# An encoder block on one Trainium2 core: when VectorE applies a norm's gain and bias, and when it prepares one pair of hidden tiles

## The chip, the core and the metric

The kernel runs on one core of a Trainium2 chip. The metric is the device time of one execution in microseconds: 1099.08 us is the median of three runs of the kernel before (1098.75 to 1099.74).

The engines are named as in the profile: PE is TensorE (PEld its weight loads), DVE VectorE, ACT ScalarE, POOL GpSimd, SP the engine whose queue issues the DMAs.

## The reference, cut to what matters

One post-norm transformer layer on 256 tokens of width 2048, all in float32:

```python
mix = hybrid_mixer(x, ...)
x = layer_norm(ALPHA * x + mix, ln1_g, ln1_b)
mem_n = layer_norm(mem, mem_ln_g, mem_ln_b)
xa = memory_cross_attention(x, mem_n, ...)
x = layer_norm(ALPHA * x + xa, ln2_g, ln2_b)
ff = jnp.square(jax.nn.relu(x @ w_mlp_in)) @ w_mlp_out     # 2048 -> 8192 -> 2048
x = layer_norm(ALPHA * x + ff, ln3_g, ln3_b)
```

The change lies in the MLP `ff` and in the residual `ALPHA * x`, where x is the second norm's output.

## The kernel before, in words

**Precision.** A float32 weight is used as the sum of a high and a low half. `queued_split` (L954) makes the halves of a piece of 1024 (or 512) columns: ScalarE writes the high half `w_hi` (L955), VectorE the low half `lo` as weight minus high half (L956). A product is three matmuls (`mm3`, L163): L164 takes the high half, L165 the low half, L166 the high half with the low half of the other operand. The high halves have a ring of four buffers (`wsp`), the low halves four fixed ones.

**Hidden tiles and units.** The hidden layer has 64 tiles of 128 columns. The first eight are made in two *groups of column tiles* (`hidden_group`, L977), four at a time; each group reads eight pieces of weights, and after each piece of the second group `pump` takes two entries from the list `side`. All other tiles come from `hidden_tile` (L1009), one at a time: two pieces of weights (`part`, L958), per piece eight matmuls with the high half and eight with the low half. Two neighbouring tiles are a *pair*. A *unit* ("u", c, q, p) multiplies pair p of chunk c with its rows of the second weight matrix, for half q of the output columns. There are four chunks (c) and two halves (q): eight passes (`one_pass`, L1060) of eight units. Units 0 to 5 of all passes but the last use seven products in place of eight: one unit has four parts (1024, 512, 1024 and 1024 columns) and 21 matmuls, and needs sums of weight blocks (`push_sums`, L942, three VectorE operations into `s_t`) and sums of the pair's blocks. Units 6 and 7 use plain products.

**A pair's steps.** `stages` (L877) returns four: x1 `square` (ScalarE: relu and square, L883, L884), x2 `halve` (ScalarE L874, VectorE L875), x3 `add` (VectorE L894, L897, L898: the sums of blocks), x4 `halve_sums` (L874, L875 again, on the sums). Below, a1 to a4 and b1 to b4 are those of a group's first and second pair. Ahead of them each tile is evacuated from its bank (`evacuate`, L868: ScalarE L870, VectorE L871).

**The order of items.** `items` (L908) lists tiles and units: in the pass (0, 0) tiles 8, 9, unit 0, tile 10, unit 1, tile 11, unit 2, and so on; in later passes a tile ahead of each unit at first. The tiles made in pass (c, 1) belong to the next chunk. `fetch` (L919) loads each item's 1 MB of weights into a ring of buffers: four, and five from the item `JOIN` on, when the buffer `row_b` joins. Before, JOIN is unit 5 of the pass (0, 1).

**What sets the order on an engine.** `queue` (L105) chains an instruction to the one queued before it on the same engine: queued instructions run in the order in which they are emitted. What is not queued is free, and is put between the others by the scheduler. Splits, matmuls, the sums of weight blocks and the row operations are queued; merges, evacuations of single tiles and the steps of most pairs are free. `part` takes work from three lists after each split: from `banks` if there is any, and then from `sums`, or, if that is empty, from `banks` or `side` (`pump`, L114).

**The row operations.** `norm_ops(q)` (L1183) multiplies the residual `res[b]`, both blocks b of 128 tokens, by the gain of the second norm and adds its bias, for 1024 columns: four VectorE operations of 128x1024 (L1186). Their rows come into `row_b` by two DMAs (`norm_rows`, L1178). Half 0 is needed before the first pass' results are merged into `res`, half 1 before the second's. Before, half 0 was done in `side`: two operations in the second group, two in the first pass (`rows[2:]`), then the loads of half 1, whose four operations were in `side` at the start of the pass (0, 1).

**Merges.** When a pass' six seven-product units are done, `banks` gets eight operations (L1126) that add the accumulated products `p1, p5, p6, p7` into `res`; they are taken by the parts of the last two tiles and of unit 6. The four x accumulators are merged at the end of the pass (L1152).

**A pair in a pass.** After its second tile, `hidden_tile` puts the pair's four steps into `late_finish` (L1036); they are emitted after the next unit, or ahead of the next tile, whichever comes first, and are free except for the last pair of a chunk.

Of the kernel before, what the change touches and what calls it, by code (L numbers as in the profile page):

```python
# [15 lines left out]
ALU = mybir.AluOpType  # L16
# [22 lines left out]
def encoder_kernel(ctx: ExitStack, tc: tile.TileContext, t, out):  # L39
# [24 lines left out]
    def acc_tile():  # L64
        return psA.tile([P, 512], F32, tag="acc", name="acc")

    def att_tile():
        return psT.tile([P, 512], F32, tag="att", name="att")
# [33 lines left out]
    side, banks, fixed_lo = deque(), deque(), deque()  # L102
# [174 lines left out]
    cq = attA[:, 6144:8192].rearrange("p (k c) -> p k c", c=512)  # L277
# [178 lines left out]
    for b in range(NB):  # L456
# [3 lines left out]
        a, c, e = krn[:, 0:64], krn[:, 64:128], krn[:, 256:512]  # L460
        nc.vector.tensor_tensor(out=a, in0=v, in1=krt[:, 0, b, :], op=ALU.mult)
        for i in range(2):
            j = 1 - i
# [372 lines left out]
    LEAD = CH // 2  # L836
# [8 lines left out]
    m_t = late.tile([P, 512], F32, name="m_t")  # L845
# [62 lines left out]
    items = []  # L908
    for c, q in PASSES:
# [3 lines left out]
        for u in us:  # L913
            n = 2 if q == 0 and u[3] == (CH // 2 - 2 if c else 0) else 1
            items += gs[:n] + [u]
            gs = gs[n:]
    JOIN = items.index(("u", 0, 1, 5))

    def fetch():  # L919

# [7 lines left out]
        elif n:  # L928
            raws.append(row_b if n == JOIN else raws[n - (4 if n < JOIN else 5)])
        raw = raw_of[it] = raws[n]  # L930
# [4 lines left out]
        nc.sync.dma_start(raw, src)  # L935
        if n == JOIN:
            fetch()
# [39 lines left out]
    def hidden_group(nexts, tiles, c, j0, beside=None):  # L977
# [22 lines left out]
        def empty(i, h):  # L1000
            for j in range(2):
                evacuate(outs[2 * i + j], h, j, queue)

        todo = [stages(h, c, j0 // 2 + i, queue) for i, h in pairs]
        return [lambda i=i, h=h: empty(i, h) for i, h in pairs], todo

    now, late_finish = [], []

    def hidden_tile(it, ps):  # L1009

        _, c, j = it
        for h_ in range(2):
            hi, lo = part(raw_of[it][:, h_ * 1024:(h_ + 1) * 1024])
            k0 = 8 * h_

            def w_hi(k):
                queue(nc.tensor.matmul(ps, hi[:, k * P:(k + 1) * P], x2t[:, k0 + k, :],  # L1017
                                       start=k0 + k == 0, stop=k0 + k == KT - 1))

            for k in range(7):  # L1020
                w_hi(k)
            if h_ == 0:
                w_hi(7)
            for k in range(8):
                queue(nc.tensor.matmul(ps[:, 0:S], lo[:, k * P:(k + 1) * P], x2t[:, k0 + k, 0:S],  # L1025
                                       start=False, stop=False))
            if h_ == 1:
                w_hi(7)
        if j % 2 == 0:
            now[:] = [tmp_tile()]  # L1030
        evacuate(ps, now[0], j % 2)
        if j % 2:
            def rest(h=now[0]):
                for stage in stages(h, c, j // 2, queue if j == CH - 1 else free_order):
                    stage()
            late_finish.append(rest)  # L1036

    bank = []
    at = [0]
# [20 lines left out]
    def one_pass(c, q):  # L1060
# [17 lines left out]
        r11, r12, r21, r22 = [res[b][:, cc] for b in range(NB) for cc in cols]  # L1078
# [3 lines left out]
        def merge(r, x, op=ALU.add):  # L1082
            if any(r is y for y in fresh):
                fresh[:] = [y for y in fresh if y is not r]
                nc.vector.scalar_tensor_tensor(out=r, in0=r, scalar=ALPHA, in1=x, op0=ALU.mult, op1=op)
            else:
                nc.vector.tensor_tensor(out=r, in0=r, in1=x, op=op)  # L1087

        def more(ps, op=ALU.add):
            nc.vector.tensor_tensor(out=m_t, in0=m_t, in1=ps, op=op)  # L1090

        spare, n_seven, n_unit, parts = [], 0, 0, []
        while n_unit < len(order):
            it = step()
            if it[0] == "g":
                if n_unit == 0:
                    ps = {LEAD: x22, LEAD + 1: x21}[it[2]] if it[1] == 0 else p6
                elif n_seven < len(sevens):
                    ps = x22
                else:  # L1100
                    spare = spare or [p1, p6]
                    ps = spare[0]
                    spare.reverse()
                hidden_tile(it, ps)
                continue
            p, raw, k = it[3], raw_of[it], 2 * it[3]
            n_unit += 1
            if p in sevens:
                if n_seven == 0:
                    while banks:  # L1110
                        banks.popleft()()
                while sums:
                    sums.popleft()()
                for src, todo in ((raw[:, 512:1536], ((p1, a(c, k, 0)), (x12, sm(c, p, 3)))),
                                  (raw[:, 1536:2048], ((x11, a(c, k + 1, 0)),)),
                                  (s_t[:, 0:1024], ((p5, sm(c, p, 1)), (p7, sm(c, p, 0)))),
                                  (s_t[:, 1024:2048], ((p6, sm(c, p, 2)), (x21, a(c, k + 1, 1))))):
                    for (hi, lo), (ps, x) in zip(halves(part(src)), todo):
                        mm(ps, x, hi, lo)
                n_seven += 1  # L1120
                if at[0] < len(items) and is_seven(items[at[0]]):
                    push_sums(items[at[0]])
                if n_seven == len(sevens):
                    nc.scalar.activation(m_t, p1, AF.Copy)

                    banks.extend([lambda: merge(r11, m_t), lambda: more(p6),  # L1126
                                  lambda: merge(r12, m_t, ALU.subtract), lambda: more(p7, ALU.subtract),
                                  lambda: merge(r21, m_t), lambda: merge(r22, m_t, ALU.subtract),
                                  lambda: merge(r22, p5), lambda: merge(r12, p5)])
            elif final and len(order) - n_unit < HELD:  # L1130
                n = len(parts) // 2
                for i in range(2):
                    o = (2 * n + i) * 1024
                    lo = sums_h[2 * n + i - 1] if n + i else lo_tile()
                    w = halves(part(raw[:, i * 1024:(i + 1) * 1024], wide[:, o:o + 1024], lo))
                    parts.append((k + i, w))
                    for (hi, lo), ps in zip(w, (x12, x11)):
                        mm(ps, a(c, k + i, 0), hi, lo)
            else:
                for i in range(2):  # L1140
                    w = halves(part(raw[:, i * 1024:(i + 1) * 1024]))
                    for (hi, lo), to in zip(w, ((x12, x22), (x11, x21))):
                        for b in range(2):
                            mm(to[b], a(c, k + i, b), hi, lo)
            if q == 1:
                give("h", c, p)
                if p in SEVEN:
                    give("s", c, p)
            if late_finish:
                late_finish.pop()()  # L1150
# [27 lines left out]
    def norm_rows(q):  # L1178
        for i, w in enumerate("gb"):
            nc.sync.dma_start(row_b[:, i * 1024:(i + 1) * 1024],  # L1180
                              t[f"ln2_{w}"][q * 1024:(q + 1) * 1024].partition_broadcast(P))

    def norm_ops(q):  # L1183
        o = q * 1024
        return [lambda i=i, b=b, op=op: queue(
            nc.vector.tensor_tensor(out=res[b][:, o:o + 1024], in0=res[b][:, o:o + 1024],  # L1186
                                    in1=row_b[:, i * 1024:(i + 1) * 1024], op=op))
            for i, op in enumerate((ALU.mult, ALU.add)) for b in range(NB)]

    for g in range(LEAD // G):  # L1190
        empty, (first, second) = hidden_group((lambda k: w_mi0[k // 2]) if g == 0 else (lambda k: s_in.next()),
                     att_tile if g % 2 else acc_tile, 0, g * G, first_pair if g == 0 else None)
        wait = [lambda: None]

        def both(*todo):
            return [lambda: [x() for x in todo]]

        if g == 0:
            norm_rows(0)
            rows = norm_ops(0)  # L1200
            (a1, a2, a3, a4), (b1, b2, b3, b4) = first, second
            side.extend(wait * 4 + empty + [a1, b1, a3, a2, a4, b3, b2, rows[0], b4, rows[1]])
            s_in.split, s_in.beside = queued_split, 2
        else:
            (a1, a2, a3, a4), (b1, b2, b3, b4) = first, second
            assert not side
            side.extend(wait + both(*empty) + [a1] + both(a3, a2) + [a4, b1] + both(b3, b2) + [b4] + rows[2:] + [lambda: norm_rows(1)])
    bank[:] = [acc_tile() for _ in range(4)] + [att_tile() for _ in range(4)]
    for cq in PASSES:
        if cq == (0, 1):  # L1210
            side.extend(norm_ops(1))
        one_pass(*cq)

    g3, b3 = s_t, raw_of[items[-5]]
# [137 lines left out]
```

## Time and profile before

| What | Value |
|---|---|
| three runs, median (lowest, highest) | 1099.08 us (1098.75, 1099.74) |
| the profiled execution's time | 1098.77 us |
| its span, first to last instruction | 1097.0 us |
| granted TensorE clock over the span | 0.996 |
| groups of column tiles (MLP's start) | from about 399 us |
| passes (0, 0) and (0, 1) | from 446.6 and 535.5 us |
| row operations (L1186) | 439.2 to 547 us |

The times in the trace count from the first instruction. In timelines a row gives start, duration (of several merged instructions together), engine, line, operation, what is written and read, the count, and in brackets the idle time of the engine just before, with what ended it. In groups (x count) the numbers are the busy time in total, the mean of one in ns, and idle time. VectorE's rows overlap a little: an instruction begins before the one before it has ended.

### The profile page before, as it was taken

The page shows a single profiled execution, that of the slowest core. Times are in us where ns is not written, and L with a number is a line of the kernel's source. Part 1 is how long each engine was busy: PE and PEld are TensorE (multiplying, and loading weights), DVE is VectorE, ACT ScalarE, POOL GpSimd, SP SyncE. Part 2 cuts the span into 40 slices and gives each one's busy share as a digit, 9 for nine tenths or more (in the row PEclk, how much of TensorE's full clock was granted, in tenths as well). Part 3 has the DMA queues.
Part 4 walks back from the last instruction along what each step waited for, and adds up shares of the span by engine and source line. Part 5 has one row for each costly group of instructions (what it writes and reads, how often), then busy time and mean ns, then how long its engine had stood idle before and what let it go on. Part 6 is the DMA issues. An engine that isn't in the chain of part 4 may idle for free.

```text
span 1097.0 us, 15276 instructions
## 1 busy us (share of the span) xinstructions
PE 1078.5 (98%) x5864; PEld 932.4 (85%) x5864; DVE 936.8 (85%) x1299; ACT 638.4 (58%) x925; POOL 35.6 (3%) x45
## 2 busy tenths in 40 slices
PE   9999999999999999999999999999999999999996
PEld 6988899988999878878888888888888888888885
DVE  6878677678879677899999999899999899999876
ACT  6555566546576426657567557466566566666640
POOL 2402000000100000000000000000000000000000
PEclk9999999999999999999999999999999999999998
DMA  9664453466567444555565555646546555655632
GB/s 330 243 230 137 152 192 135 159 244 224 183 221 251 145 148 172 194 209 197 190 242 207 203 186 201 220 168 223 201 183 229 193 192 202 220 180 194 250 143 78
DMA packets 37369, 215.87 MB, mean 197 GB/s; under 512 B 4272, under 2 KB 5168, under 8 KB 13616
## 3 DMA queue, kind: packets, MB, share of 16 engines
q1 hardware_dynamic: 37296, 214.89, 55.0%
q8 instruction: 46, 0.75, 0.3%
q14 instruction: 27, 0.22, 0.1%
HBM read 212.78 MB, written 2.10 MB: 196 GB/s over the span
## 4 chain that ended last, share of the span: by engine, by line
PE 93%; DVE 5%; ACT 1%; issue 1%; DMA 0%; POOL 0%; DVEq 0%; SPq 0%
PE acc L164 13%; PE acc L165 13%; PE acc L166 13%; PE acc L1017 12%; PE acc L1025 6%; PE att L1017 6%; PE att L165 4%; PE att L166 4%; PE att L164 4%; PE att L1025 3%; PE acc L206 2%; PE acc L204 2%; PE acc L205 2%; DVE lo L956 1%; PE acc L213 1%; PE att L213 1%
## 5 line engine op out<-in xcount | busy, mean ns | idle before, releaser
L88 DVE TENSOR_TENSOR w_lo<-raw,w_hi 128x1024 fp32r<-128x1024 f32 (+2 forms) x130 | 147.4, 1142 | 60.1 <-ACT w_hi L87 59.1
L87 ACT ACTIVATE w_hi<-raw 128x1024 fp32r<-128x1024 f32 (+2 forms) x134 | 131.5, 989 | 114.3 <-PE acc L166 71.6
L956 DVE TENSOR_TENSOR lo<-raw,w_hi 128x1024 fp32r<-128x1024 f32 (+1 forms) x154 | 171.3, 1130 | 9.1 <-ACT w_hi L955 8.8
L955 ACT ACTIVATE w_hi<-raw 128x1024 fp32r<-128x1024 f32 (+1 forms) x154 | 147.6, 983 | 29.8 <-PE acc L166 26.3
L1017 PE MATMUL acc<-x2t,w_hi 128*128 128x512 f32 x592 | 153.3, 391 | 0.0
L1017 PEld LDWEIGHTS acc<-x2t,w_hi 128*128 128x128 f32 x592 | 108.9, 189 | 19.6
L956 DVE TENSOR_TENSOR lo<-s_t,w_hi 128x1024 fp32r<-128x1024 f32 x84 | 102.5, 1220 | 11.2 <-ACT w_hi L955 10.9
L955 ACT ACTIVATE w_hi<-s_t 128x1024 fp32r<-128x1024 f32 x84 | 88.7, 1057 | 35.6 <-PE acc L1017 13.5
L1025 PEld LDWEIGHTS acc<-x2t,lo 128*128 128x128 f32 x592 | 80.8, 190 | 5.8
L165 PE MATMUL acc<-lo,ht 128*128 128x512 f32 x213 | 83.0, 390 | 1.4 <-DVE lo L956 1.4
L1025 PE MATMUL acc<-x2t,lo 128*128 128x256 f32 x592 | 82.5, 282 | 0.0
L164 PE MATMUL acc<-w_hi,ht 128*128 128x512 f32 x210 | 82.0, 390 | 0.2 <-DVE res L1087 0.2
L166 PE MATMUL acc<-w_hi,ht 128*128 128x512 f32 x210 | 81.8, 389 | 0.0
L1017 PE MATMUL att<-x2t,w_hi 128*128 128x512 f32 x304 | 78.4, 391 | 0.0
L870 ACT ACTIVATE tmp<-acc 128x256 f32<-128x256 f32 x41 | 15.4, 385 | 99.0 <-PE acc L1017 94.7
L166 PE MATMUL acc<-w_hi,xt 128*128 128x512 f32 (+2 forms) x192 | 69.6, 364 | 0.0
L165 PE MATMUL acc<-w_lo,xt 128*128 128x512 f32 (+2 forms) x192 | 69.4, 363 | 0.0
L164 PE MATMUL acc<-w_hi,xt 128*128 128x512 f32 (+2 forms) x192 | 66.4, 366 | 0.7 <-ACT w_hi L87 0.7
L1017 PEld LDWEIGHTS att<-x2t,w_hi 128*128 128x128 f32 x304 | 55.7, 189 | 10.0
L956 DVE TENSOR_TENSOR lo<-raw_x,w_hi 128x1024 fp32r<-128x1024 f32 (+1 forms) x50 | 55.3, 1124 | 1.9 <-ACT w_hi L955 1.9
L955 ACT ACTIVATE w_hi<-raw_x 128x1024 fp32r<-128x1024 f32 (+1 forms) x50 | 47.9, 976 | 10.2 <-PE acc L166 5.2
L165 PE MATMUL att<-lo,aux 128*128 128x512 f32 x131 | 51.9, 396 | 1.3 <-DVE lo L956 1.3
(293 smaller groups left out, 2504.7 us busy)
## 6 DMA issues: line engine op xcount, KB each, us to landing
raw<-in_w_mo SPq DMA_DIRECT2D x41, 1024.0 KB, 4.8
raw<-in_w_mc SPq DMA_DIRECT2D x34, 1024.0 KB, 4.8
raw<-in_w_out SPq DMA_DIRECT2D x16, 1024.0 KB, 4.9
raw_x<-in_w_mc SPq DMA_DIRECT2D x13, 1024.0 KB, 4.8
raw_x<-in_w_mo SPq DMA_DIRECT2D x13, 1024.0 KB, 4.8
row_b<-in_w_mo SPq DMA_DIRECT2D x10, 1024.0 KB, 4.9
row_b<-in_w_mc SPq DMA_DIRECT2D x9, 1024.0 KB, 4.9
raw<-in_w_mi SPq DMA_DIRECT2D x8, 1024.0 KB, 4.8
```

Of the source, the lines that this page charges most:

```text
L87: pin(nc.scalar.activation(hi, src, AF.Copy), pinned)
L88: return pin(nc.vector.tensor_tensor(out=lo, in0=src, in1=f(hi), op=ALU.subtract), pinned)
L164: keep(nc.tensor.matmul(ps, ah, bh, start=start, stop=False))
L165: keep(nc.tensor.matmul(ps, ah, bl, start=False, stop=False))
L166: keep(nc.tensor.matmul(ps, al, bh, start=False, stop=stop))
L204: nc.tensor.matmul(ps, hi, xt[:, k, 0:S], start=k == 0, stop=False)
L205: nc.tensor.matmul(ps, hi, xt[:, k, S:2 * S], start=False, stop=False)
L206: nc.tensor.matmul(ps, lo, xt[:, k, 0:S], start=False, stop=k == nk - 1)
L955: queue(nc.scalar.activation(hi, src, AF.Copy))
L956: queue(nc.vector.tensor_tensor(out=lo, in0=src, in1=f(hi), op=ALU.subtract))
L1017: queue(nc.tensor.matmul(ps, hi[:, k * P:(k + 1) * P], x2t[:, k0 + k, :], start=k0 + k == 0, stop=k0 + k == KT - 1))
L1025: queue(nc.tensor.matmul(ps[:, 0:S], lo[:, k * P:(k + 1) * P], x2t[:, k0 + k, 0:S], start=False, stop=False))
```

## The change

Four things change.

- The list `side` of the second group: b2 with the first row operation and b4 with the second are now one entry each (`both`), and the other two operations of half 0 (`rows[2:]`) follow in the same group. Before, they stood behind the second group's own steps, in the first pass.
- The loads of half 1 (`norm_rows(1)`) are emitted right behind the second group, no longer as an entry of `side`.
- The four row operations of half 1 leave `side` and go into `banks` at the end of the pass (0, 1): the two of token block 0 ahead of the eight merges, the two of block 1 between the fourth and the fifth. So `row_b` comes free later, and `JOIN` is now unit 0 of the pass (1, 0), six items later.
- The pair of tiles 8 and 9 (chunk 0), the first whose tiles are made within a pass, does not go into `late_finish` any more: its steps go into `side` as three entries (x1; x3 and x2; x4) behind the second group's, and are queued.

`both` itself only moves from the loop over the groups to a place ahead of `hidden_tile`.

```diff
@@ -914,7 +914,7 @@
-    JOIN = items.index(("u", 0, 1, 5))
+    JOIN = items.index(("u", 1, 0, 0))
@@ -1004,6 +1004,9 @@
+    def both(*todo):
+        return [lambda: [x() for x in todo]]
+
@@ -1033,7 +1036,11 @@
             def rest(h=now[0]):
                 for stage in stages(h, c, j // 2, queue if j == CH - 1 else free_order):
                     stage()
-            late_finish.append(rest)
+            if (c, j) == (0, LEAD + 1):
+                x1, x2, x3, x4 = stages(now[0], c, j // 2, queue)
+                side.extend([x1] + both(x3, x2) + [x4])
+            else:
+                late_finish.append(rest)
@@ -1123,8 +1130,9 @@
                     nc.scalar.activation(m_t, p1, AF.Copy)
 
-                    banks.extend([lambda: merge(r11, m_t), lambda: more(p6),
-                                  lambda: merge(r12, m_t, ALU.subtract), lambda: more(p7, ALU.subtract),
+                    rows0, rows1 = late_rows[(c, q)] if (c, q) in late_rows else ([], [])
+                    banks.extend(rows0 + [lambda: merge(r11, m_t), lambda: more(p6),
+                                  lambda: merge(r12, m_t, ALU.subtract), lambda: more(p7, ALU.subtract)] + rows1 + [
                                   lambda: merge(r21, m_t), lambda: merge(r22, m_t, ALU.subtract),
                                   lambda: merge(r22, p5), lambda: merge(r12, p5)])
@@ -1192,23 +1200,22 @@
-        def both(*todo):
-            return [lambda: [x() for x in todo]]
-
         if g == 0:
             norm_rows(0)
             rows = norm_ops(0)
             (a1, a2, a3, a4), (b1, b2, b3, b4) = first, second
-            side.extend(wait * 4 + empty + [a1, b1, a3, a2, a4, b3, b2, rows[0], b4, rows[1]])
+            side.extend(wait * 4 + empty + [a1, b1, a3, a2, a4, b3] + both(b2, rows[0])
+                        + both(b4, rows[1]) + rows[2:])
             s_in.split, s_in.beside = queued_split, 2
         else:
             (a1, a2, a3, a4), (b1, b2, b3, b4) = first, second
             assert not side
-            side.extend(wait + both(*empty) + [a1] + both(a3, a2) + [a4, b1] + both(b3, b2) + [b4] + rows[2:] + [lambda: norm_rows(1)])
+            side.extend(wait + both(*empty) + [a1] + both(a3, a2) + [a4, b1] + both(b3, b2) + [b4])
+            norm_rows(1)
     bank[:] = [acc_tile() for _ in range(4)] + [att_tile() for _ in range(4)]
+    n1 = norm_ops(1)
+    late_rows = {(0, 1): (n1[0::2], n1[1::2])}
     for cq in PASSES:
-        if cq == (0, 1):
-            side.extend(norm_ops(1))
         one_pass(*cq)
```

## The prediction

> **What bounds the kernel now.** The page comes first: TensorE is busy nearly all the time, and the chain that ended last is TensorE's.
>
> ```profile
> PE 1078.5 (98%) x5864; PEld 932.4 (85%) x5864; DVE 936.8 (85%) x1299; ACT 638.4 (58%) x925; POOL 35.6 (3%) x45
> ...
> PE 93%; DVE 5%; ACT 1%; issue 1%; DMA 0%; POOL 0%; DVEq 0%; SPq 0%
> ```
>
> So there is something to win only where TensorE waits. The view of PE's waits says where in the code (waiting line, releaser: total us, times, longest):
>
> ```profile
> PE att L165 <- DVE lo L956: 1.7, 3, 0.8
> ...
> PE acc L165 <- DVE lo L956: 1.4, 1, 1.4
> ```
>
> L165 is the second matmul of a term, the first that needs the low half of the weights; L956 makes that half on VectorE. PE's timeline puts these four waits into two units: unit 1 of the first pass, begun at 468.12, and unit 0 of the second. Its last two rows here show an undisturbed unit from first matmul to the next tile:
>
> ```profile
> 468.12 0.40 PE L164 MATMUL att<-w_hi,ht 128*128 128x512 f32 x1
> 468.88 0.50 PE L165 MATMUL att<-lo,ht 128*128 128x512 f32 x1 [0.36 <-DVE lo L956]
> ...
> 471.95 0.50 PE L165 MATMUL acc<-lo,ht 128*128 128x512 f32 x1 [1.44 <-DVE lo L956]
> ...
> 473.69 0.80 PE L165 MATMUL att<-lo,aux 128*128 128x512 f32 x1 [0.77 <-DVE lo L956]
> ...
> 545.91 0.51 PE L165 MATMUL att<-lo,aux 128*128 128x512 f32 x1 [0.57 <-DVE lo L956]
> ...
> 594.17 0.40 PE L164 MATMUL att<-w_hi,ht 128*128 128x512 f32 x1
> ...
> 598.95 1.98 PE L1017 MATMUL att<-x2t,w_hi 128*128 128x512 f32 x8
> ```
>
> The windows price them. Each stretch but the third is one hidden tile and one unit, the same work (columns: length; busy PE, PEld, DVE, ACT, POOL; granted clock; DMA share; GB/s):
>
> ```profile
> 462.55:477.65 15.10, 12.54 (x55) 9.65 (x53) 15.10 (x23) 9.74 (x14) 0.00 (x0) 0.89 0.40 141
> 477.65:487.99 10.34, 10.34 (x54) 8.86 (x53) 10.31 (x12) 6.22 (x8) 0.00 (x0) 1.00 0.73 254
> 473.69:477.65 3.96, 3.96 (x12) 3.20 (x12) 3.96 (x4) 2.52 (x3) 0.00 (x0) 0.63 0.56 232
> 535.50:547.16 11.66, 10.94 (x54) 8.70 (x53) 11.66 (x15) 6.10 (x7) 0.00 (x0) 1.00 0.51 180
> ```
>
> An undisturbed stretch takes 10.34 us, and VectorE works through 10.31 of it: it is nearly a second bound, so whatever is put on it here shows. The first stretch loses 15.10 - 10.34 = 4.76 us: 0.36 + 1.44 + 0.77 = 2.57 are waits, about (1 - 0.63) x 3.96 = 1.5 the lower clock that followed, the rest restarts. The fourth loses 11.66 - 10.34 = 1.32. More than 4.76 + 1.32 = 6.1 us the change cannot give back.
>
> The Trainium skill, "TensorE: Matmul & The Clock Gate", table under "Why this matters for your kernels", says that the clock falls after an idle gap of over about 3 us. The trace differs: the longest gap is 1.44 us, and behind it the clock was 0.63. By that sentence no lower clock could come after the change, and the worse end of part 2's price and one rival below would fall away; by the rows several short waits close together suffice, and I go by the rows.
>
> **Part 1: two of the first four row operations leave the first pass.** What VectorE does around unit 1:
>
> ```profile
> L1186 DVE TENSOR_TENSOR res<-res,row_b 128x1024 f32<-128x1024 f32 x8 | 9.8, 1220 | 0.0
> 443.19 2.36 DVE L956 TENSOR_TENSOR lo<-raw_x,w_hi 128x1024 fp32r<-128x1024 f32 x2
> 446.54 1.42 DVE L871 TENSOR_TENSOR tmp<-att,tmp 128x256 f32<-128x256 f32 x4 [0.99 <-ACT tmp L870]
> ...
> 453.74 1.82 DVE L956 TENSOR_TENSOR lo<-raw,w_hi 128x1024 fp32r<-128x1024 f32 x2
> 455.48 0.42 DVE L894 TENSOR_TENSOR tmp<-tmp 128x256 f32<-128x256 f32 x1
> ...
> 457.07 1.22 DVE L956 TENSOR_TENSOR lo<-s_t,w_hi 128x1024 fp32r<-128x1024 f32 x1
> ...
> 461.84 1.23 DVE L956 TENSOR_TENSOR lo<-raw,w_hi 128x1024 fp32r<-128x1024 f32 x1 [1.28 <-ACT w_hi L955]
> ...
> 467.60 1.22 DVE L956 TENSOR_TENSOR lo<-raw_x,w_hi 128x1024 fp32r<-128x1024 f32 x1
> ...
> 472.41 1.22 DVE L956 TENSOR_TENSOR lo<-s_t,w_hi 128x1024 fp32r<-128x1024 f32 x1
> 473.55 1.22 DVE L1186 TENSOR_TENSOR res<-res,row_b 128x1024 f32<-128x1024 f32 x1
> ...
> 475.82 1.22 DVE L1186 TENSOR_TENSOR res<-res,row_b 128x1024 f32<-128x1024 f32 x1
> ```
>
> An operation of 1024 elements lets the next begin after 1.14 us (472.41 to 473.55), one of 512 after 0.60 (453.74: 1.82 for both sizes, less 1.22). The two row operations of 473.55 and 475.82, 2 x 1.14 = 2.27 us, go to the end of the second group of column tiles. So the first pass' first low halves, begun at 443.19, are ready 2.27 later, at 445.46 + 2.36 = 447.8. TensorE starts this pass at 462.55 less two tiles of 5.56 (10.34 - 4.78; a unit is 598.95 - 594.17 = 4.78) and a unit, 446.65, and wants the first low half 8 matmuls on, at 448.5: covered. The group's own last low half gets a halving and a row operation ahead of it that stood behind it, between it and 443.19: it ends at about 443.3 instead of 441.5, and TensorE reads it in the last 2 us before 446.65; covered too. VectorE's idle times of 0.99 at 446.54 and 1.28 at 461.84 then swallow the 2.27. Cost: 0; without this cover, at most 2.27.
>
> The row loads of the other half (L1180) now stand on SP's queue ahead of the pass' fetches and wait for the last of these operations, to about 445.5. The fetch behind them waits for the low half that ends at 447.8 anyway. And JOIN, six items later, only keeps the ring at four buffers, as in the first 27 items, for which no wait of PE above names a DMA. Both 0.
>
> **Part 2: the pair of tiles 8 and 9.** Its steps were free after unit 0 and ran among the last steps of the group. They now stand in the queues, behind the third and fourth part of unit 1 and the first of unit 2. ScalarE there:
>
> ```profile
> 459.20 1.14 ACT L883 ACTIVATE tmp<-tmp 128x512 f32<-128x512 f32 x2
> 460.24 0.62 ACT L884 ACTIVATE tmp<-tmp 128x512 f32<-128x512 f32 x1
> 460.76 2.00 ACT L955 ACTIVATE w_hi<-raw 128x1024 fp32r<-128x1024 f32 x2
> ...
> 470.73 0.63 ACT L874 ACTIVATE aux<-tmp 128x512 fp32r<-128x512 f32 x1 [1.04 <-DVE tmp L898]
> ```
>
> I replay unit 1 by hand with these spacings. One square fewer at 459.20, so the split of 460.76 comes 0.37 earlier (the two that stay depend on each other); between 461.84 and 467.60 a halving (0.60) and two sums (0.53) of the pair go. VectorE thus begins unit 1 at 467.60 - 0.37 - 1.13 = 466.1. Then the group's last pair steps (455.48 to 457.07: 1.59): part 2 begins at 466.1 + 1.14 + 1.59 = 468.8, ready at 469.5. A unit is 21 matmuls, 4.78 / 21 = 0.2275 each; part 2's low half is the eighth, wanted at 468.12 + 7 x 0.2275 = 469.7: just in time. Then a halving 0.60 and an evacuation 0.33: part 3 begins at 470.3, ready at 471.5, wanted at 470.4: **late by 1.15**. ScalarE is close behind: the halving of 470.73 waits for the group's sums and now comes at 468.6, so part 3's high half ends at 470.2; the pair's relu and square (1.2) stand before part 4's, which ends at 472.3, its low half at 473.6, wanted 6 matmuls after part 3's, at 473.0: **late by 0.55 more**. Unit 1 loses 1.7. In unit 2 VectorE carries the other pair steps, 1.59 and 0.60; by the same count its parts 1 and 3 are late by 0.35 and 0.65: **1.0**. From unit 3 on none.
>
> Gain of the first pass: 4.76 - 1.7 - 1.0 = 2.06, say **2.0 us**. Ends: were ScalarE never in the way, VectorE's work alone would leave about 1.4 of waiting: gain 3.3. With the lower clock again, 1.5 less: 0.5. I take the middle value, since it follows the order of the queues.
>
> **Part 3: the other four row operations** leave unit 0 of the second pass, with 4 x 1.14 = 4.5 us of VectorE; the wait at 545.91 goes: **gain 1.3**. They come back at the end of that pass, two behind the first half of tile 6 and two behind unit 6, with the merges of the same rows behind them. There VectorE's lead over TensorE grows: it begins unit 5 at 591.86 for a unit of 594.17, 2.3 ahead, and the next pass' unit 0 5.4 ahead:
>
> ```profile
> 591.86 1.82 DVE L956 TENSOR_TENSOR lo<-row_b,w_hi 128x1024 fp32r<-128x1024 f32 x2
> ...
> 621.18 1.22 DVE L956 TENSOR_TENSOR lo<-raw,w_hi 128x1024 fp32r<-128x1024 f32 x1
> 626.57 0.40 PE L164 MATMUL att<-w_hi,aux 128*128 128x512 f32 x1
> ```
>
> A unit begins without waits with a lead of about 1 (1.14 for its first low half, wanted 0.23 in). Putting 4.5 us in leaves 5.4 - 4.5 = 0.9 and VectorE's idle time there on top: it just fits at the end, and inside the last two tiles and units one part may come late. Between 0 and 1.5 us; I take **0.4**, nearer the fit.
>
> Sum: 2.0 + 1.3 - 0.4 = 2.9 us. The profiled execution took 1098.77 (span 1097.0), so 1095.9; the median stands 0.3 above it: **1096.2**.
>
> **The rivals.** *Short waits pull the clock down again.* 1.15 and 0.55 within 3 us come near the 1.44 and 0.77 that did it; against it, they are a fifth to a third shorter. Price 1.5, of which VectorE wins back some 0.5 of lead: gain 1.9, 1097.2. *ScalarE is not in the way*: the sums of the group could be done earlier; gain 3.3 + 1.3 - 0.2 = 4.4, 1094.7. *Nothing much comes of it*: the queued pair holds up as much as the row operations did, or the tail takes 1.5: gain about 1, 1098.1. *Slower*: in the second pass' tail the four operations stand in the queue in front of low halves that TensorE wants, and the merges behind them; if none of the 4.5 is hidden and the clock falls, 4.5 + 1.5 = 6.0 against 3.3 gained: 1101.8. It decides from 3.3 us of waiting in the tail on; the lead of 5.4 speaks against it.
>
> **How the numbers follow.** Forecast 0.50, clock 0.16, ScalarE free 0.16, little 0.13, slower 0.05. Under 0.2%, 2.2 us, is about what a measurement here cannot tell from no change. Faster by more, below 1096.9: 0.46 of the forecast's 0.50 and ScalarE's 0.16, together 0.62; slower 0.05; same 0.33. The range takes in the ends, 3.3 + 1.3 - 0 = 4.6 and 0.5 + 1.3 - 1.5 = 0.3: 1094.5 to 1098.8, which leaves out about 0.15.
>
> **What would show it.** Right: no row operation on VectorE between 470 and 478 nor in the second pass' unit 0, that stretch 10.34 long; waits of PE for `lo` in units 1 and 2 under 3 us together, clock 1.00 throughout. Wrong: a granted clock under 1 near 475, unit 1 as long as before, or new waits of L165 or L1017 near 600 to 620, or a `row_b` load that lets a tile wait.

## The result, and the profile after

The change made the kernel slower: 1105.14 us (median of 6 runs, 1104.46 to 1106.42) against 1099.41 us (median of 6, 1098.75 to 1100.87), a ratio of 1.0052, 95% interval 1.004 to 1.0065. Forecast were 1096.2 us and a range of 1094.5 to 1098.8. The profiled execution took 1104.50 us, its span is 1102.7.

First the page after the change, the lines that answer to those of before. TensorE is no more idle in the large. The chain has 2% of DMA, but these are four loads in its first 27 us, far ahead of the change, and kernels below that are no slower than before start with such loads too (pair_only, evac_fixed). Nothing here says where the 5.7 us by which the span grew went.

```profile
PE 1080.1 (98%) x5864; PEld 931.2 (84%) x5864; DVE 936.3 (85%) x1299; ACT 638.4 (58%) x925; POOL 38.2 (3%) x45
...
PE 92%; DVE 4%; DMA 2%; ACT 1%; issue 0%; SPq 0%; POOL 0%; DVEq 0%; ACTq 0%
```

The waits of PE after (L1094 is the addition in `merge`, L1087 before):

```profile
PE acc L164 <- DVE res L1094: 3.8, 2, 3.5
PE att L165 <- DVE lo L956: 2.3, 4, 0.9
...
PE acc L165 <- DVE lo L956: 1.1, 1, 1.1
```

There is a new wait of 3.5 us, in which a product waits for a merge, and the waits for low halves have not gone: five times, 3.4 us in all, against four times 3.1 before. PE's timeline after gives their places:

```profile
461.75 0.50 PE L165 MATMUL att<-lo,aux 128*128 128x512 f32 x1 [0.91 <-DVE lo L956]
...
473.14 0.50 PE L165 MATMUL acc<-lo,ht 128*128 128x512 f32 x1 [1.06 <-DVE lo L956]
...
474.88 0.50 PE L165 MATMUL att<-lo,aux 128*128 128x512 f32 x1 [0.77 <-DVE lo L956]
...
476.94 0.50 PE L165 MATMUL att<-lo,aux 128*128 128x512 f32 x1 [0.41 <-DVE lo L956]
...
484.40 0.50 PE L165 MATMUL att<-lo,ht 128*128 128x512 f32 x1 [0.19 <-DVE lo L956]
...
631.13 0.79 PE L164 MATMUL acc<-w_hi,aux 128*128 128x512 f32 x1 [3.52 <-DVE res L1094]
```

The first four stand in units 0 and 1 of the first pass, the fifth in unit 2, the last in unit 0 of the pass (1, 0). The same stretches as in the prediction, in windows (first two tiles and unit 0; units 1 and 2; unit 0 of (0, 1); unit 0 of (1, 0); the 3.4 us behind its wait; columns as there, the granted clock third from the end):

```profile
447.23:464.74 17.51, 16.52 (x86) 13.62 (x85) 15.12 (x23) 12.29 (x20) 0.00 (x0) 1.00 0.65 240
464.74:478.23 13.49, 11.26 (x55) 8.62 (x54) 11.61 (x19) 8.57 (x13) 0.00 (x0) 1.00 0.45 157
478.23:489.47 11.24, 11.04 (x54) 8.63 (x53) 11.21 (x14) 7.80 (x11) 0.00 (x0) 1.00 0.52 181
537.05:547.39 10.34, 10.34 (x54) 8.86 (x53) 9.12 (x12) 6.11 (x7) 0.00 (x0) 1.00 0.60 216
621.18:636.82 15.64, 12.12 (x54) 9.85 (x53) 13.71 (x21) 7.35 (x9) 0.00 (x0) 0.89 0.34 125
631.13:634.50 3.37, 3.37 (x8) 2.68 (x9) 1.44 (x3) 2.04 (x3) 0.00 (x0) 0.53 0.00 0
```

Against before (15.93, 15.10, 10.34; 11.66; 10.35): unit 0 of the first pass lost 1.58, unit 1 won 1.61, unit 2 lost 0.90; unit 0 of (0, 1) won 1.32; unit 0 of (1, 0) lost 5.29. With the stretches next to them that is 4.9 of the span's 5.7. Another 0.6 lies ahead of the first pass (447.23 against 446.62); it is there already 50 us earlier (a matmul at 397.88 against 397.23), ahead of all code that the change touches, and so is none of its doing. So two things have to be explained: why the first pass won nothing, and the 5.29.

**The first pass.** VectorE after, in units 0 and 1 (L894, L897 and L898 are the three sums of a pair, L871 the evacuation of a tile):

```profile
456.82 0.42 DVE L894 TENSOR_TENSOR tmp<-tmp 128x256 f32<-128x256 f32 x1
459.00 0.42 DVE L871 TENSOR_TENSOR tmp<-acc,tmp 128x256 f32<-128x256 f32 x1 [1.76 <-ACT tmp L870]
459.34 0.28 DVE L897 TENSOR_TENSOR tmp<-tmp 128x128 f32<-128x128 f32 x1
...
469.61 0.42 DVE L894 TENSOR_TENSOR tmp<-tmp 128x256 f32<-128x256 f32 x1
470.93 0.42 DVE L871 TENSOR_TENSOR tmp<-acc,tmp 128x256 f32<-128x256 f32 x1 [0.90 <-ACT tmp L870]
471.27 0.28 DVE L897 TENSOR_TENSOR tmp<-tmp 128x128 f32<-128x128 f32 x1
```

An evacuation stands between two sums of a pair. Each time it waits for the half that ScalarE copies (L870) when TensorE has ended the tile, so VectorE, busy for nearly the whole of a stretch, stands idle for 1.76 and 0.90 us. Before, in the same two units:

```profile
455.93 0.29 DVE L897 TENSOR_TENSOR tmp<-tmp 128x128 f32<-128x128 f32 x1
456.26 0.29 DVE L898 TENSOR_TENSOR tmp<-tmp 128x128 f32<-128x128 f32 x1
...
458.81 0.42 DVE L871 TENSOR_TENSOR tmp<-acc,tmp 128x256 f32<-128x256 f32 x1
...
468.94 0.42 DVE L894 TENSOR_TENSOR tmp<-tmp 128x256 f32<-128x256 f32 x1
469.27 0.42 DVE L871 TENSOR_TENSOR tmp<-acc,tmp 128x256 f32<-128x256 f32 x1
469.61 0.28 DVE L897 TENSOR_TENSOR tmp<-tmp 128x128 f32<-128x128 f32 x1
```

In unit 0 the three sums ran without a break from 455.48, and the evacuation came behind the pair's last halving. Nothing in the diff touches the evacuation: it is free, and the scheduler put it elsewhere. In unit 1 the evacuation stood between the same two sums before, and cost nothing there: the tile was done when VectorE came to it. After the change its place is the old one, but VectorE comes to it ahead of TensorE.

**The pass (1, 0).** VectorE after, from the row operations (L1194) to the merge that TensorE waits for (L1092 and L1094 are merges, L1097 an addition into `m_t`):

```profile
598.49 2.48 DVE L1194 TENSOR_TENSOR res<-res,row_b 128x1024 f32<-128x1024 f32 x2
...
608.10 1.22 DVE L1194 TENSOR_TENSOR res<-res,row_b 128x1024 f32<-128x1024 f32 x1
...
612.84 0.68 DVE L1092 SCALAR_TENSOR_TENSOR res<-res,m_t 128x512 f32<-128x512 f32 x1
...
617.45 0.68 DVE L1097 TENSOR_TENSOR m_t<-m_t,att 128x512 f32<-128x512 f32 x1
...
620.12 1.28 DVE L1092 SCALAR_TENSOR_TENSOR res<-res,m_t 128x512 f32<-128x512 f32 x2
...
625.79 1.27 DVE L1094 TENSOR_TENSOR res<-res,att 128x512 f32<-128x512 f32 x2
626.99 0.28 DVE L897 TENSOR_TENSOR tmp<-tmp 128x128 f32<-128x128 f32 x1
627.19 1.22 DVE L956 TENSOR_TENSOR lo<-s_t,w_hi 128x1024 fp32r<-128x1024 f32 x1
...
629.79 1.28 DVE L1094 TENSOR_TENSOR res<-res,acc 128x512 f32<-128x512 f32 x2
```

This is one chain, for each link changes or reads `m_t` or the same rows of `res`: rows, m_t, res, p5, and at last the accumulators x22 and x12 (629.79). The merges are free, the splits between them are queued and went ahead. TensorE's unit 0 needs x12 empty for its fourth matmul, at 627.4; it got it at 631.13. The clock then fell to 0.53, and 3.52 us of waiting became 5.29. Before, with no row operations at the head of the chain, the merges with p5 came 15 us earlier:

```profile
610.70 1.28 DVE L1087 TENSOR_TENSOR res<-res,att 128x512 f32<-128x512 f32 x2
```

### The profile page after: what moved, and what is told of

The parts are those of the page before. It is cut to its first block, busy times and chain, and to the rows that moved or that the text cites. A ratio compares the mean times of both kernels' runs of the same rounds, so it can differ in the third digit from the quotient of the medians.

```text
span 1102.7 us, 15271 instructions
## 1 busy us (share of the span) xinstructions
PE 1080.1 (98%) x5864; PEld 931.2 (84%) x5864; DVE 936.3 (85%) x1299; ACT 638.4 (58%) x925; POOL 38.2 (3%) x45
## 4 chain that ended last, share of the span: by engine, by line
PE 92%; DVE 4%; DMA 2%; ACT 1%; issue 0%; SPq 0%; POOL 0%; DVEq 0%; ACTq 0%
PE acc L164 13%; PE acc L165 12%; PE acc L166 12%; PE acc L1020 12%; PE acc L1028 6%; PE att L1020 6%; PE att L165 4%; PE att L166 4%; PE att L164 4%; PE att L1028 3%; PE acc L206 2%; PE acc L204 2%; PE acc L205 2%; DVE lo L956 1%; PE acc L213 1%; PE att L213 1%
## 5 line engine op out<-in xcount | busy, mean ns | idle before, releaser
L870 ACT ACTIVATE tmp<-acc 128x256 f32<-128x256 f32 x41 | 15.4, 385 | 101.9 <-PE acc L1020 97.6
L166 PE MATMUL acc<-w_hi,ot 128*128 128x512 f32 (+1 forms) x136 | 51.9, 382 | 0.0
```

Source lines behind the costliest of these rows:

```text
L166: keep(nc.tensor.matmul(ps, al, bh, start=False, stop=stop))
```

## The experiments

The lengths of the stretches, start of a tile to start of the next, from PE's timeline; ratios to the kernel before with 95% intervals. "Tail" is tile 6 and unit 6 of the pass (0, 1).

| Kernel | first pass, units 0, 1, 2 | (0, 1) unit 0 | tail | (1, 0) unit 0 | ratio |
|---|---|---|---|---|---|
| before | 15.93, 15.10, 10.34 | 11.66 | 11.02 | 10.35 | |
| the change | 17.51, 13.49, 11.24 | 10.34 | 11.02 | 15.64 | 1.0052 (1.004 to 1.0065) |
| tail_only | 15.94, 15.15, 10.35 | 10.35 | 11.03 | 15.77 | 1.0034 (1.0021 to 1.0047) |
| first_only | 17.52, 13.45, 11.25 | 11.65 | 11.02 | 10.35 | 1.0007 (0.9998 to 1.0016) |
| evac_fixed | 15.94, 12.45, 11.25 | 11.67 | 11.03 | 10.35 | 0.9985 (0.9976 to 0.9994) |
| tail_queued | 17.51, 13.45, 11.26 | 10.34 | 12.75 | 10.35 | 1.001 (1.0001 to 1.002) |
| rows_only | 17.52, 13.44, 10.34 | 11.67 | 11.03 | 10.34 | 1.0001 (0.9992 to 1.001) |
| pair_only | 15.94, 14.34, 11.00 | 11.68 | 11.03 | 10.34 | 1.0002 (0.9993 to 1.0011) |
| spread | 15.93, 12.46, 11.27 | 10.35 | 11.03 | 10.35 | 0.999 (0.9981 to 0.9998) |
| spread_pair | 15.93, 11.60, 11.63 | 10.35 | 11.03 | 10.34 | 0.9981 (0.9972 to 0.999) |
| both_fixed | 15.94, 12.44, 11.28 | 10.34 | 12.77 | 10.34 | 0.9993 (0.9984 to 1.0002) |
| split_rows | 15.94, 11.58, 11.61 | 10.53 | 11.88 | 10.35 | 0.9981 (0.9972 to 0.999) |

### Each half of the change alone

tail_only, the second half's part on the kernel before:

```diff
-    JOIN = items.index(("u", 0, 1, 5))
+    JOIN = items.index(("u", 1, 0, 0))
...
-                    banks.extend([lambda: merge(r11, m_t), lambda: more(p6),
-                                  lambda: merge(r12, m_t, ALU.subtract), lambda: more(p7, ALU.subtract),
+                    rows0, rows1 = late_rows[(c, q)] if (c, q) in late_rows else ([], [])
+                    banks.extend(rows0 + [lambda: merge(r11, m_t), lambda: more(p6),
+                                  lambda: merge(r12, m_t, ALU.subtract), lambda: more(p7, ALU.subtract)] + rows1 + [
...
+    n1 = norm_ops(1)
+    late_rows = {(0, 1): (n1[0::2], n1[1::2])}
     for cq in PASSES:
-        if cq == (0, 1):
-            side.extend(norm_ops(1))
```

> The kernel before with only the second half's four row operations moved into the end of the pass (0, 1), and JOIN six items later; the first pass is as before. Theory M (the accumulators of the pass (0, 1) are merged too late because the row operations stand in front of the chain of merges): the stretch of unit 0 of (0, 1) goes from 11.66 to 10.34, the first stretch of (1, 0) from 10.35 to about 15.6 with a wait of PE for a merge of about 3.5 us; together +3.9 us, 1103.2. Rival W (all the loss comes from VectorE's work in the first pass, and the late merge is its echo): both stretches at 10.34, 1098.

Measured: 10.35 and 15.77, as theory M has it, a ratio of 1.0034. The first pass is that of before, so W falls: the late merge is no echo of it.

first_only is the changed kernel with these lines undone.

> The changed kernel with the second half's row operations and JOIN as before; only the first pass is changed. Theory M: the first three stretches stay as in the changed kernel (17.5, 13.5, 11.2: 0.9 more than before), the stretch of unit 0 of (0, 1) is 11.66 again and the first of (1, 0) 10.35: 1100.2. Rival W: the late merge of (1, 0) remains, 1104 or more.

Measured: the first pass of the changed kernel to 0.04 us, the pass (1, 0) undisturbed at 10.35, the ratio 1.0007: this half of the change neither won nor lost anything that the runs can tell apart from nothing. The profile shows it 0.9 behind.

### The order on VectorE

evac_fixed is first_only with the evacuations of tiles 9 and 10 queued behind the third part of units 0 and 1. For tile 9 that is the place of before; the prediction's replay had tile 10's a little earlier, ahead of the third part:

```diff
-    now, late_finish = [], []
+    now, late_finish, kept_evac = [], [], []
+
+    def flush():
+        kept_evac.pop()()
...
-        evacuate(ps, now[0], j % 2)
+        if c == 0 and j in (LEAD + 1, LEAD + 2):
+            kept_evac.append(lambda h=now[0]: evacuate(ps, h, j % 2, queue))
+        else:
+            evacuate(ps, now[0], j % 2)
...
-                side.extend([x1] + both(x3, x2) + [x4])
+                side.extend(both(x1, flush) + both(x3, x2) + [x4])
...
-            side.extend(wait + both(*empty) + [a1] + both(a3, a2) + [a4, b1] + both(b3, b2) + [b4])
+            side.extend(wait + both(*empty) + [a1] + both(a3, a2) + both(a4, flush) + [b1] + both(b3, b2) + [b4])
```

> As first_only, but the evacuations of tiles 9 and 10 are queued, behind the third part of units 0 and 1: the order on VectorE that the prediction reckoned with. Theory E (a free evacuation was put ahead of the sums of a pair, and VectorE stood idle 1.76 and 0.90 us for TensorE to end the tile): the three stretches lose about 2.7 us in all instead of 5.7 against 15.92 + 10.34 + 10.34, so about 3 us less than first_only: 1097.3. Rival W (VectorE has too much work there whatever the order): within 0.5 us of first_only.

Measured: 1097.76 us against 1100.59 for first_only. VectorE of evac_fixed in unit 0, with no idle time in front of any of these:

```profile
458.53 0.41 DVE L894 TENSOR_TENSOR tmp<-tmp 128x256 f32<-128x256 f32 x1
458.98 0.29 DVE L897 TENSOR_TENSOR tmp<-tmp 128x128 f32<-128x128 f32 x1
...
461.85 0.42 DVE L871 TENSOR_TENSOR tmp<-acc,tmp 128x256 f32<-128x256 f32 x1
462.18 1.21 DVE L956 TENSOR_TENSOR lo<-s_t,w_hi 128x1024 fp32r<-128x1024 f32 x1
```

Unit 0 is back at 15.94 and unit 1 at 12.45: 17.52 + 13.45 - 15.94 - 12.45 = 2.58 us for the place of two evacuations. Theory E holds, W does not. The three stretches sum up to 39.64, 1.73 less than before.

Which part of the diff brought the idle times? rows_only moves the first half's row operations (and the loads of half 1 behind them) and leaves the pair free; pair_only queues the pair and leaves the operations where they were.

The edit of rows_only, against first_only:

```diff
-            if (c, j) == (0, LEAD + 1):
-                x1, x2, x3, x4 = stages(now[0], c, j // 2, queue)
-                side.extend([x1] + both(x3, x2) + [x4])
-            else:
-                late_finish.append(rest)
+            late_finish.append(rest)
```

> The first half's row operations in the second group and the second half's loads behind it, as in the change; the pair of tiles 8 and 9 free after unit 0, and the second half's operations and JOIN, as before. Theory E (the place of the free evacuations): moving the row operations shifts VectorE by 2.3 us, and that alone puts the evacuation of tile 9 ahead of a pair's sums, so VectorE idles there about 1.8 us and unit 0 loses 1.6 as in first_only; the three stretches together about 42: 1100. Rival Q (queueing the pair does it): the stretches of units 0 and 1 lose about 2.5 of the 4.76 of before, together 39.1: 1097.5.

The edit of pair_only, against the kernel before:

```diff
-            late_finish.append(rest)
+            if (c, j) == (0, LEAD + 1):
+                x1, x2, x3, x4 = stages(now[0], c, j // 2, queue)
+                side.extend([x1, lambda: [x3(), x2()], x4])
+            else:
+                late_finish.append(rest)
```

> The kernel before with only the pair of tiles 8 and 9 queued, behind the first half's row operations in the first pass. Theory E: unit 0 keeps its order, its stretch stays at 15.93; in unit 1 the evacuation of tile 10 stands ahead of a pair's sums, VectorE idles about 0.9 there, and units 1 and 2 together lose 4.5 to 5.5 as against 4.76: 1099 to 1100. Rival Q: unit 0 loses 1.6 here too, 1101.

```profile
460.50 0.42 DVE L871 TENSOR_TENSOR tmp<-acc,tmp 128x256 f32<-128x256 f32 x1 [1.76 <-ACT tmp L870]
...
448.72:466.24 17.52, 16.54 (x87) 13.62 (x85) 15.38 (x25) 12.86 (x21) 0.00 (x0) 1.00 0.69 243
466.24:479.68 13.44, 11.24 (x55) 8.62 (x54) 13.40 (x20) 9.18 (x13) 0.00 (x0) 1.00 0.46 158
```

These are the evacuation of tile 9 and the windows of rows_only: unit 0 loses 1.59 with the row operations moved and the pair left alone, as E has it, and in pair_only it loses nothing (15.94). So Q falls for unit 0. For unit 1 it is the other way round: rows_only has no idle time before tile 10's evacuation, and pair_only has one of 0.97, with its place as before. pair_only wins 0.76 in unit 1 and loses 0.66 in unit 2 and 0.58 in unit 3 (10.93, not in the table).

In rows_only two operations moved into the stage before, where they end at 447.7, 11 us ahead of the evacuation, cost 1.59 in unit 0 and won 1.66 in unit 1: moving them was worth nothing while a third instruction changed its place. What they alone win with that place kept was not run; evac_fixed, with the pair queued too, wins 1.73. Why the scheduler placed tile 9's evacuation so stays open; only that it did is shown.

### The tail with the merges in order

tail_queued is the changed kernel with the eight merges of the pass (0, 1) queued where they are emitted (`kept[0]` stands around the instructions in `merge` and `more`):

```diff
+                    kept[0] = queue if (c, q) in late_rows else free_order
...
         if not final:
+            kept[0] = free_order
```

> The changed kernel with the eight merges of the pass (0, 1) queued in the order in which they are emitted, so that the splits of the following tiles cannot pass them. Theory M: the merges with p5 come before the end of the pass, the accumulator x12 is free in time, the first stretch of (1, 0) falls from 15.64 to 10.4, or to 11 if a low half then comes late in the last two tiles: 1099.5 to 1100.5. Rival J (the later JOIN or the later load of row_b holds unit 0 of (1, 0) up): 15.6 stays, 1105.

Measured: JOIN and the load of `row_b` are those of the change, and the first stretch of (1, 0) is 10.35: M holds, J falls. VectorE, the merges with p5 and then those of two of the accumulators:

```profile
615.54 1.28 DVE L1096 TENSOR_TENSOR res<-res,att 128x512 f32<-128x512 f32 x2
...
623.94 1.28 DVE L1096 TENSOR_TENSOR res<-res,acc 128x512 f32<-128x512 f32 x2
```

The merges with p5 come 10 us earlier than in the change (625.79), and no product waits for x12. But the price shows up elsewhere, in unit 6 of the tail, where low halves come late:

```profile
606.18 0.50 PE L165 MATMUL acc<-lo,ht 128*128 128x512 f32 x1 [0.54 <-DVE lo L956]
...
609.81 0.50 PE L165 MATMUL acc<-lo,ht 128*128 128x512 f32 x1 [0.61 <-DVE lo L956]
```

The tail takes 12.75 instead of 11.02: 1.73 lost, against the 1.37 that unit 0 and its neighbour win. In this order too, the move of the second half is no gain. The kernel took 1100.84 us, a little above the 1099.5 to 1100.5 that M allowed.

both_fixed has both mends, evac_fixed's and tail_queued's:

> The change with both orders kept: the evacuations of tiles 9 and 10 queued as in evac_fixed, the eight merges queued as in tail_queued. If the two causes are separate they add up: the first three stretches 39.64 as in evac_fixed, unit 0 of (0, 1) 10.34, the tail's stretch 12.75 and the first of (1, 0) 10.35 as in tail_queued: 1.73 + 1.38 - 1.72 = 1.4 us less than before, 1098.2. If not: VectorE, now ahead in the first pass, has other orders in the second and the tail loses more, 1099 to 1100.

Measured: 39.66, 10.34, 12.77, 10.34: each stretch is that of its own mend to 0.03 us, so the two causes are separate. The ratio, 0.9993, cannot be told from 1; expected was 0.9987, which its interval takes in.

### Where the row operations fit

spread is evac_fixed with the second half's operations one to a unit:

```diff
-            side.extend(norm_ops(1))
+            side.extend([x for op in norm_ops(1) for x in wait * 3 + [op]])
```

> evac_fixed with the second half's four row operations one in each of units 0 to 3 of the pass (0, 1), behind the unit's fourth part. Theory L (one operation of 1.14 us fits into VectorE's lead of 3 us at unit 0, which shrinks by about 0.7 a unit; four at once do not fit): the stretch of unit 0 falls from 11.67 to 10.34 and the next three stay at 10.35, 0.2 at most: 1.3 less than evac_fixed, 1096.4. Rival (VectorE has no room in this pass at all): the loss of 1.3 only moves to units 1 to 3, 1097.8.

Its windows, units 0, 2, 3 and 4 of (0, 1):

```profile
536.89:547.24 10.35, 10.35 (x55) 8.86 (x53) 9.14 (x12) 6.10 (x7) 0.00 (x0) 1.00 0.56 203
557.59:568.38 10.79, 10.67 (x55) 8.75 (x53) 10.79 (x16) 7.75 (x11) 0.00 (x0) 1.00 0.58 194
568.38:579.39 11.01, 10.67 (x54) 8.78 (x53) 10.98 (x13) 6.25 (x8) 0.00 (x0) 1.00 0.53 190
579.39:590.64 11.25, 10.69 (x54) 8.77 (x53) 11.25 (x16) 7.92 (x11) 0.00 (x0) 1.00 0.79 282
```

Unit 0 is free of waits, and units 2 to 4 lose 0.45 + 0.66 + 0.90 = 2.0, more than the four operations cost together at unit 0 (1.32). Theory L falls. Its rival is nearer, though it had 1.3 of loss and in units 1 to 3: VectorE, busy for the whole of the last three stretches, has no room there.

spread_pair, made from spread, puts the pair's queued steps into unit 2 alone:

```diff
-                side.extend(both(x1, flush) + both(x3, x2) + [x4])
+                side.extend([flush, lambda: None, x1] + both(x3, x2) + [x4])
```

> spread with the queued steps of the pair of tiles 8 and 9 in unit 2 alone (its first three parts), so that ScalarE's relu and square no longer stand ahead of unit 1's fourth part. Theory S (ScalarE's queue order makes part of unit 1's wait): unit 1's second wait of 0.7 goes, unit 2 has both pairs and loses 0.5 more: the three stretches 39.6 to 39.1, 1096. Rival (only VectorE's work counts): unit 2 or 3 loses what unit 1 gains, within 0.3 of spread.

Measured: unit 1 falls from 12.46 to 11.60, unit 2 rises from 11.27 to 11.63: 0.50 won, as S has it. The pair's sums and its halving on VectorE moved with ScalarE's two operations, so what each of them cost is not separated.

split_rows has spread_pair's first pass, two operations in unit 0 of (0, 1), and two in the tail among merges that are queued as in tail_queued. The lines on the row operations, against the changed kernel:

```diff
-    late_rows = {(0, 1): (n1[0::2], n1[1::2])}
+    late_rows = {(0, 1): ([], n1[1::2])}
     for cq in PASSES:
+        if cq == (0, 1):
+            side.extend(n1[0::2])
```

> spread_pair's first pass; of the second half's row operations the two of token block 0 stay in unit 0 of the pass (0, 1), where VectorE's lead is 3 us, and the two of block 1 are in the tail, between the queued merges, where it grows to 5.4. Theory L (each place takes about two operations, 2.27 us, for nearly nothing, and four cost 1.4 to 1.7): unit 0's stretch 10.4, the tail's 11.0 to 11.3: the first pass' 2.2 and 1.0 to 1.3 less than before, 1096.2. Rival (any operation in either place costs in proportion): unit 0 about 11.0 and the tail about 11.9, 1097.3.

```profile
535.97:546.50 10.53, 10.53 (x54) 8.70 (x53) 10.53 (x14) 6.10 (x7) 0.00 (x0) 1.00 0.58 199
598.24:610.12 11.88, 11.34 (x57) 9.34 (x56) 11.78 (x18) 6.45 (x9) 0.00 (x0) 1.00 0.46 168
```

Two operations at unit 0 cost 0.19 where four cost 1.32: there L is right. In the tail two cost 0.86 where four cost 1.73: in proportion, and L is wrong. The proportion also speaks against the queueing of the merges as the tail's price, though queued merges without row operations were not run. One of the eleven executions of split_rows took 6152 us; its ratio is that of the others. With spread_pair this is the fastest version, 0.9981 (0.9972 to 0.999) of the kernel before, about 2 us.

## Why the prediction was wrong

- **Part 1, "Cost: 0": wrong.** Its sum was right: no low half came late at the pass' start. What failed is what it took for granted, that instructions which are not queued keep their places when the work around them moves by 2.3 us. Of its idle times of 0.99 and 1.28 only 0.30 was left, but a new one of 1.76 us came in front of the evacuation of tile 9, and unit 0 lost 1.58.
- **Part 2, the replay of units 1 and 2: close, where the order is kept.** It gave 1.7 + 1.0 us of loss; evac_fixed, with nearly its order, loses 12.45 - 10.34 = 2.11 and 11.25 - 10.34 = 0.91. Gain 1.73 against 2.0 forecast. One of its steps is off by itself: six matmuls behind 471.5 is 472.9 and not 473.0, so by its own numbers part 4 is late by 0.7 and not 0.55. In the kernel as built VectorE stood idle for 0.90 before tile 10's evacuation, which the replay does not have, and the first pass lost about 0.9.
- **Part 3, "gain 1.3" at unit 0 of (0, 1): right**, 1.32 and 0.05 in its neighbour.
- **Part 3, "it just fits", 0.4: wrong, and the costliest step.** It counted the lead of VectorE's low halves over TensorE, and nothing else that TensorE waits for. The row operations stand at the head of a chain of merges at whose end an accumulator comes free, and the next pass' unit 0 needs it within its first four matmuls. The prediction has no such deadline. Cost as built 5.29; with the merges in order 1.73, above the 1.5 that was its bound, and then for the reason given, a late low half.
- **The rivals.** "Slower" had the work in the right place, the second pass' tail, and a price of 6.0 near the 5.29, and "the merges behind them" among its words; but the wait came in the next pass, it put the wait on low halves, and the 4.5 of its price are row operations that nothing hides, where the 5.29 are 3.52 of waiting for one accumulator and a lower clock behind it. That the two prices are near each other is luck. "Short waits pull the clock down again" did not come in the first pass: 1.00 there, with waits of 1.06 and 0.77.
- **JOIN and the row loads at 0: right**, by tail_queued, which has both and an undisturbed pass (1, 0).
- **The clock: one reading was wrong.** The prediction calls 1.44 us the longest gap in the trace before. TensorE's view of waits has one of 1.6 (1.57 at 399.45), behind which the clock stayed at 1.00. So waits of this size need not lower the clock (last section).
- **The signs.** Those of being right came true where it looked: unit 0 of (0, 1) took 10.34, and the waits in units 1 and 2 came to 2.43 us, under 3, at a clock of 1.00. The losses lay in unit 0 of the first pass and in the pass (1, 0), for which it had named no sign.

## What to carry to other kernels

Before an edit that moves work on a nearly full engine, list which instructions around it have no fixed place, and ask of each what it waits for: one of them, put a step too early, can cost as much as the move of the work wins (here 1.59 against 1.66 us). For a result that must be cleared before its buffer is used again, follow the whole chain from the moved instruction to the clearing and set it against the first use, not against the average lead of the engine. Where a place is right by reckoning, fix it in the program instead of leaving it to the scheduler.

## What the runs showed of the hardware

Equal waits leave the clock alone in one execution and lower it in another. Windows ahead of the first pass, over nearly the same code (evac_fixed is 0.74 us behind), in the profile of the kernel before and of evac_fixed; in both TensorE had just waited 0.71 and 1.57 us:

```profile
401.00:406.00 5.00, 5.00 (x34) 4.38 (x33) 3.74 (x8) 2.21 (x4) 0.00 (x0) 1.00 0.34 109
```

```profile
401.00:406.00 5.00, 5.00 (x23) 4.29 (x22) 2.89 (x7) 1.13 (x2) 0.00 (x0) 0.67 0.23 65
```

Here 34 matmuls at full clock, there 23 at 0.67. pair_only, 0.11 us behind evac_fixed at that place, had the full clock too. In six of the twelve profiles the window has a clock of 1.00 and the first pass begins at 446.6 to 447.8 us; in the six others it has 0.66 to 0.73, and the pass begins at 448.6 to 449.7. first_only and rows_only have the same code up to there and stand on different sides. This is why stretches were compared here, and not spans. Later it shows again, with waits that are not quite equal: those of 1.06, 0.77 and 0.41 in unit 1 left the changed kernel at a clock of 1.00, and 1.05 and 0.77 brought pair_only's unit 1 to 0.88:

```profile
463.41:477.75 14.34, 12.52 (x55) 9.90 (x53) 13.30 (x18) 7.68 (x10) 0.00 (x0) 0.88 0.40 148
```

The Trainium skill, "TensorE: Matmul & The Clock Gate", section "What's actually happening", says that the activity of TensorE is judged in a window that runs freely, not started by the kernel; that would let equal waits end differently, as they do here. No run here shows the window itself.
